# Shifting the lower weight parts of an MLP's first product by 224 bytes in SBUF

## The chip, the cores and the metric

The kernel runs on one core of one Trainium2 chip. The metric is device time in microseconds (us), from the start to the end of one execution. Before the change three runs gave a median of 1940.86 us (1940.85 to 1940.98).

## The reference

The program is a trunk of two layers on 256 tokens with 2048 features, in float32. Layer 0 mixes tokens with a convolution module, layer 1 with multi-head latent attention. Each mixer is followed by an MLP with squared ReLU; every sub-layer has an RMS norm ahead of it and a residual add behind it, and one last RMS norm ends the program.

```python
for layer in range(DEPTH):                       # DEPTH = 2
    h = rms_norm(x, norm_mixer_g[layer])
    x = x + (conv_module if layer % 2 == 0 else mla)(h, ...)
    h = rms_norm(x, norm_mlp_g[layer])
    x = x + jnp.square(jax.nn.relu(h @ w1)) @ w2  # w1: 2048 x 8192, w2: 8192 x 2048
return rms_norm(x, final_norm_g)
```

The change is about `h @ w1`, the up product of the MLP, which both layers compute.

## The kernel before

**Products in parts.** A float32 product is made from one-pass matmuls in the type float32r. Each operand is split into a higher part (the value rounded by a copy to float32r, on ScalarE) and a lower part (the value minus the higher part, on VectorE or GpSimd). Three products are added: higher by higher, lower by higher, higher by lower. The tiles of the weights' parts are called `hi` and `lo`; there are six buffers of each (`WB`), in one pool, 4096 bytes per partition each. A matmul has a stationary operand, which a weight load (LDWEIGHTS, PEld in the profile) brings into the array ahead of it, and a moving operand that streams through. The profile names them in the order moving, stationary: `acc<-xt,lo` streams tokens past lower weight parts.

**The up product** (lines 487 to 520) runs on weights that arrive in units of 128 columns and all 2048 rows, 8192 bytes per partition. A unit is cut into two chunks of eight blocks of 128 x 128. For each block the weights are stationary and the tokens move: one matmul with `hi` on 512 columns (line 510: the tokens' higher and lower parts stand side by side in the tiles `xt`), and one with `lo` on the 256 columns of the tokens' higher parts (line 508). The first chunk of a unit runs its eight `hi`, then its eight `lo`; the second chunk its eight `lo`, then its eight `hi`. So sixteen `lo` matmuls follow each other, then eight `hi`, then the next work. Each layer has 64 such units; a layer's count of matmuls on line 508 is 1024, on line 510 also 1024.

**The down product** has the activations stationary and the weight parts `hi` and `lo` moving, 512 columns at a time (`mm3`, lines 195 to 197). `stream` (from line 423) runs over the chunks of both products in an order written out beforehand. For each chunk it first prepares parts up to six chunks ahead (`prep`, which calls `split_into`, lines 420 and 421), then issues the matmuls. When a raw unit has been read by its last split, the next load starts. TensorE, ScalarE and VectorE work in the order of this code.

**The other places.** The convolution's first product (lines 850 to 852) has `hi` and `lo` stationary and 256 token columns moving. The down projection of attention streams 288 columns of `hi` and `lo` at a time past the tokens. `turn` (line 288) loads small vectors (norm gains, biases) by transposing staged rows and copying the result out of PSUM into `vecs` and `vecs2`. `rsqrt`, `finish` and others take small tiles from the pool `small`, which has two buffers of each unless told otherwise.

**Where the tiles lie.** Several narrow tiles named `pad_...` serve only to place what follows them. In the built program the tiles that matmuls in float32r read (`hi`, `lo`, `xt`, the activations' `sh` and `sl`, the parts in attention) all begin at 64 modulo 256 bytes in their partition, and so does each block of 128 x 128 in them, since a block is 512 bytes. Only the second half of the 288 moving columns in attention's down projection begins at 192.

Of the kernel before, what the change touches and what calls it, by code (L numbers as in the profile page):

```python
# [10 lines left out]
F32 = mybir.dt.float32  # L11
F32R = mybir.dt.float32r
# [6 lines left out]
P = 128  # L19
D = 2048  # L20
KC = D // P
T = 2
S = T * P
FF = 4 * D
NB = 512
NNB = D // NB
# [6 lines left out]
QR = 512  # L33
# [1 line left out]
CHUNK = 64  # L35
PARTS = 4
PAD_CONST = 24
PAD_SMALL = 32
PAD_RIGHT = 40
PAD_SH = 16  # L40
PAD_STATS = 48
PAD_O = 64
WB = 6
# [39 lines left out]
def trunk_kernel(  # L83
# [29 lines left out]
    const = ctx.enter_context(tc.tile_pool(name="const", bufs=1))  # L113
    main = ctx.enter_context(tc.tile_pool(name="main", bufs=1))
    wpool = ctx.enter_context(tc.tile_pool(name="wpool", bufs=2))
    small = ctx.enter_context(tc.tile_pool(name="small", bufs=2))
    psum, psum_cx = {}, [ExitStack()]

    def repool(name, **banks):
# [19 lines left out]
    def nm(s):  # L139
        uid[0] += 1  # L140
        return f"{s}_{uid[0]}"
# [70 lines left out]
    def rsqrt(ms, n, eps, name):  # L212

        v = small.tile([P, n], F32, tag=f"v{name}", name=nm("v"))
        y = small.tile([P, n], F32, tag=f"y{name}", name=nm("y"))
        t = small.tile([P, n], F32, tag=f"t{name}", name=nm("t"))
        nc.vector.tensor_scalar(v, ms, scalar1=eps, scalar2=None, op0=ALU.add)
        nc.scalar.activation(t, v, AF.Sqrt)
        nc.vector.reciprocal(y, t)
        nc.vector.scalar_tensor_tensor(out=t, in0=y, scalar=-0.5, in1=y, op0=ALU.mult, op1=ALU.mult)  # L220
        nc.vector.tensor_tensor(t, t, v, op=ALU.mult)
        nc.vector.scalar_tensor_tensor(out=y, in0=t, scalar=1.5, in1=y, op0=ALU.add, op1=ALU.mult)
        return y
# [61 lines left out]
            at += r  # L285
        return stage

    def turn(dst, stage):
        n = dst.shape[-1]
        pt = tr_tile()  # L290
        nc.tensor.transpose(pt[:, :n], stage[:n, :], ident[:n, :n])
        nc.vector.tensor_copy(dst, pt[:, :n])

    n_vecs, n_vecs2 = (sum(r for _, r in v) for v in (vec_rows, vec_rows2))
    vecs = const.tile([P, n_vecs], F32, name="vecs")
    vecs2 = const.tile([P, n_vecs2], F32, name="vecs2")
    g_mix = [vecs[:, 0:KC], vecs[:, KC : 2 * KC]]
    g_mlp = [vecs[:, 2 * KC : 3 * KC], vecs[:, 3 * KC : 4 * KC]]
    b_pw1 = vecs[:, 4 * KC : 6 * KC]
    b_dw = vecs[:, 6 * KC : 7 * KC]  # L300


    xt_cx, xt = [ExitStack()], []
# [24 lines left out]
    def residual_stage(last, gain, r_scale=None):  # L328


        ssq = small.tile([P, T, NNB], F32, tag="ssq", name=nm("ssq")) if last else None

        def add(n, ps, t):
            sl = slice(n * NB, (n + 1) * NB)
            if r_scale is None:
                nc.vector.tensor_tensor(xs[:, t, sl], ps[t], xs[:, t, sl], op=ALU.add)
            else:
                nc.vector.scalar_tensor_tensor(
                    out=xs[:, t, sl], in0=ps[t], scalar=r_scale[:, t : t + 1], in1=xs[:, t, sl],
                    op0=ALU.mult, op1=ALU.add,  # L340
                )

        def prepare(n, only=None):
            sl = slice(n * NB, (n + 1) * NB)
            if last:
                if gain is not None:
                    for j in range(2):
                        to_T(xs, 4 * n + 2 * j, xh, xl, gain)
                for t in range(T) if only is None else [only]:
                    nc.scalar.activation(spare[-1](), xs[:, t, sl], AF.Square, accum_out=ssq[:, t, n : n + 1])  # L350

        return ssq, add, prepare
# [60 lines left out]
        def __init__(self, prep, run, after=(), now=None, ahead=None):  # L413
            self.prep, self.run, self.after, self.now, self.ahead = prep, run, after, now, ahead

    def hi_lo(n):
        return [wpool.tile([P, n, NB], F32R, tag=c, name=nm(c), bufs=WB) for c in ("hi", "lo")]

    def split_into(parts, src):
        nc.scalar.activation(parts[0], src, AF.Copy)  # L420
# [53 lines left out]
    def mlp(layer, ssq, next_gain, finish=None, before=None, last_w1=None):  # L474

        w1, w2 = mlp_w1[layer], mlp_w2[layer]
        r2 = small.tile([P, T], F32, tag="r2", name=nm("r2"))
        made_stage, pre, first_tiles, blocked, n_s, sums_left = [], [], {}, {}, [0], []

        def u_tile():  # L480
# [5 lines left out]
        def up_units(hs, q, p, extra):  # L486

            sevens = SEVENS[layer][q]
            held = {}
            large = p in sevens or (q == PARTS - 1 and p in LATE_G[layer])  # L490

            def up_unit(b):
                ps = []

                def chunk(h):
                    def prep(raw, parts):
                        parts[h] = [a.rearrange("p a (j n) -> p (a j) n", n=P) for a in hi_lo(2)]
                        split_into(parts[h], raw[:, 8 * h : 8 * h + 8, :])

                    def run(parts):  # L500
                        if not ps:
                            ps.append(acc_tile())
                        wh, wl = parts.pop(h)
                        for low in (h, 1 - h):
                            for j in range(8):
                                k = 8 * h + j
                                if low:
                                    nc.tensor.matmul(ps[0][:, :S], wl[:, j, :], xh(k), start=False, stop=False)  # L508
                                else:
                                    nc.tensor.matmul(ps[0], wh[:, j, :], xhl(k), start=k == 0, stop=k == KC - 1)  # L510

                    def out():
                        if b == 0:
                            held["u"] = u_tile()
                        nc.scalar.activation(held["u"][:, b, :], ps[0], AF.Copy)  # L515

                    if h == 0:
                        return Chunk(prep, run)
                    return Chunk(prep, run, [add, lambda: None, square, forms, part] + extra if b == 1 else [], now=out)

                unit = Unit(rows(w1, 0, KC, ((q * NPAIR + p) * 2 + b) * P, P), KC, [chunk(h) for h in range(2)])
                unit.last_read = 1
                return unit

            def add():
                v = held["u"][:, :, :S]
                nc.vector.tensor_tensor(v, v, held["u"][:, :, S:], op=ALU.add)

            def square():
                n_s[0] += large  # L530
                v = held["u"][:, :, :S]
                nc.scalar.activation(v, v, AF.Relu)
                if p in sevens:
                    held["f"] = f = f_tile()
                    nc.scalar.activation(f[:, 0:4, :].rearrange("p (b t) n -> p b (t n)", b=2), v, AF.Square)
                    held["src"], shape, tag, n = f[:, 1:8, :], [P, 7, P], "s", N_S
                else:
                    nc.scalar.activation(v, v, AF.Square)
                    held["src"], shape = v, [P, 2, S]
                    tag, n = ("s", N_S) if large else ("g", N_G)  # L540
                held["hl"] = [mp.tile(shape, F32R, tag=tag + c, name=nm(tag + c), bufs=n) for c in "hl"]

            def forms():
                if p in sevens:
                    f = held["f"]
                    nc.vector.tensor_tensor(
                        f[:, 4:6, :], f[:, 0:1, :].broadcast_to([P, 2, P]), f[:, 1:3, :], op=ALU.subtract
                    )
                    nc.vector.tensor_tensor(f[:, 6, :], f[:, 1, :], f[:, 5, :], op=ALU.subtract)
                    nc.vector.tensor_tensor(f[:, 7, :], f[:, 3, :], f[:, 6, :], op=ALU.subtract)  # L550

            def part():
                hs[p] = held["hl"]
                split_into(hs[p], held["src"])

            if large:
                blocked[square] = lambda: n_s[0] < N_S and not (p in sevens and sums_left)
            return [up_unit(b) for b in range(2)]
# [235 lines left out]
    with ExitStack() as cx:  # L794
# [2 lines left out]
        squares_to = cv.tile([P, NB], F32, name="squares_to")  # L797
        spare.append(lambda: squares_to)

        ln_g = vecs2[:, 0:KC]  # L800
        ln_b = vecs2[:, KC : 2 * KC]
        g_q = vecs2[:, 2 * KC : 2 * KC + QR // P]
        g_kv = vecs2[:, 2 * KC + QR // P :]
        NW = W * KC // 4
        w_dw = cv.tile([P, W * KC], F32, name="w_dw")
        vecs_rows = stage_rows(cv, vec_rows, nc.scalar)
# [1 line left out]
        b2 = cv.tile([P, D], F32, name="b2")  # L808

        cn = cv.tile([P, T, D], F32, tag="tok", name="cn")  # L810
        cv.tile([P, PAD_SH], F32, name="pad_sh")
        sh = cv.tile([P, KC, S], F32R, name="sh")
        sl_ = cv.tile([P, KC, S], F32R, name="sl_")
        cv.tile([P, PAD_STATS], F32, name="pad_stats")
# [202 lines left out]
        with tc.manual_schedule():  # L1017
# [8 lines left out]
                nc.scalar.activation(xn[:, 1, hs], xs[:, 1, hs], AF.Square, accum_out=xsq[:, h : h + 1])  # L1026
            for n in range(NNB):
                nc.vector.bn_stats(xst[:, n, :], xs[:, 0, n * NB : (n + 1) * NB])
            turn(vecs, vecs_rows)
            keep_warm(xs[:, 1, D - P :], N_WARM)  # L1030
            nc.vector.bn_aggr(xmv, xst.rearrange("p a b -> p (a b)"))
            nc.vector.tensor_tensor(ms0[:, 0:1], xmv[:, 0:1], xmv[:, 0:1], op=ALU.mult)
# [31 lines left out]
            turn0(3)  # L1064
            conv_mm(0, 4)
            conv_load(4)
            turn(vecs2, vecs2_rows)
            conv_mm(0, 8)
            pt = tr_tile()
            for i in range(4):  # L1070
# [672 lines left out]
    def before(ssq):  # L1743

        for t in range(T):
            m = small.tile([P, 1], F32, tag="msp", name=nm("msp"))
            nc.vector.tensor_reduce(m, ssq[:, t, : NNB // 2], axis=AX.X, op=ALU.add)
            nc.vector.tensor_scalar(m, m, scalar1=1.0 / D, scalar2=EPS, op0=ALU.mult, op1=ALU.add)
            part.append(m)
# [30 lines left out]
```

## Time and profile before

| | |
|---|---|
| median of three runs | 1940.86 us (1940.85 to 1940.98) |
| profiled execution | 1940.68 us, span 1938.9 us |
| granted TensorE clock, mean | 0.998 |
| matmuls, weight loads | 10778 each |
| line 510, `hi`, 512 columns | 2048 |
| line 508, `lo`, 256 columns | 2048 |

The profiled execution's own time is 0.18 us under the median; 1.8 us of it lie outside the span, which goes from the first to the last instruction. A matmul's duration in the profile is modelled and overlaps that of the next, so the cost of one in a row of matmuls is the distance from its start to the next start, called its pitch here. The shapes in a row are partitions x elements, "idle" is the time that the engine stood still just ahead of the group.

### The profile page before, as it was taken

What the parts mean: (1) busy time and instruction counts of PE and PEld (TensorE: products, weight loads), DVE (VectorE), ACT (ScalarE), POOL (GpSimd) and SP (SyncE); (2) the same over time, 40 slices, a digit from 0 to 9 for tenths busy, and PEclk for the clock granted to TensorE, in tenths of its full rate; (3) what the DMA queues carried; (4) which work ended last, traced back from release to release, by engine and by line L of the source; (5) the groups of instructions that cost most, each with busy time, mean ns of one, the idle gap of its engine ahead of it and who ended that gap; (6) DMA issues with size and microseconds to landing.
All of it is one profiled execution on the core that took longest, in us unless ns stands there. A gap on an engine that the chain in (4) does not pass through costs nothing.

```text
span 1938.9 us, 28476 instructions
## 1 busy us (share of the span) xinstructions
PE 1915.4 (99%) x10778; PEld 1682.5 (87%) x10778; DVE 1651.8 (85%) x2372; ACT 1204.8 (62%) x1709; POOL 223.7 (12%) x183
## 2 busy tenths in 40 slices
PE   7999999999999999999999999999999999999998
PEld 7999888888888888888899998888888888888886
DVE  5999875789999999999976666557999999999887
ACT  5556654766666666666566665556766666666654
POOL 5999400000000000000001410000000000000000
PEclk9999999999999999999999999999999999999999
DMA  8666456857666667666646445765667666766663
GB/s 236 184 175 177 146 184 169 222 171 210 198 204 204 203 198 212 200 198 212 199 143 182 121 152 174 200 186 171 201 191 210 210 196 195 214 200 195 211 223 109
DMA packets 407113, 367.62 MB, mean 190 GB/s; under 512 B 15416, under 2 KB 351936, under 8 KB 406720
## 3 DMA queue, kind: packets, MB, share of 16 engines
q1 hardware_dynamic: 405952, 363.63, 62.8%
q10 hardware_dynamic: 1024, 2.17, 0.3%
q8 instruction: 84, 1.38, 0.3%
q14 instruction: 53, 0.43, 0.1%
HBM read 363.68 MB, written 2.10 MB: 189 GB/s over the span
## 4 chain that ended last, share of the span: by engine, by line
PE 98%; DVE 1%; DMA 1%; ACT 0%; issue 0%; DVEq 0%; ACTq 0%
PE acc L510 24%; PE acc L196 15%; PE acc L195 15%; PE acc L197 15%; PE acc L508 13%; PE acc L851 3%; PE acc L850 3%; PE acc L852 3%; PE acc L251 1%; PE sum L900 1%; PE acc L1435 0%; PE acc L1437 0%; PE acc L1436 0%; PE acc L1412 0%; PE acc L1414 0%; PE acc L1413 0%
## 5 line engine op out<-in xcount | busy, mean ns | idle before, releaser
L421 DVE TENSOR_TENSOR lo<-raw,hi 128x1024 fp32r<-128x1024 f32 (+1 forms) x512 | 571.1, 1122 | 90.1 <-ACT hi L420 81.7
L420 ACT ACTIVATE hi<-raw 128x1024 fp32r<-128x1024 f32 (+1 forms) x512 | 479.7, 970 | 66.9 <-PE acc L196 66.6
L510 PE MATMUL acc<-xt,hi 128*128 128x512 f32 x2048 | 503.2, 391 | 0.0
L510 PEld LDWEIGHTS acc<-xt,hi 128*128 128x128 f32 x2048 | 376.1, 188 | 72.5
L195 PE MATMUL acc<-hi,sh 128*128 128x512 f32 x930 | 362.7, 390 | 0.0
L197 PE MATMUL acc<-lo,sh 128*128 128x512 f32 x930 | 362.0, 389 | 0.0
L196 PE MATMUL acc<-hi,sl 128*128 128x512 f32 x802 | 312.0, 389 | 0.0
L508 PEld LDWEIGHTS acc<-xt,lo 128*128 128x128 f32 x2048 | 262.6, 191 | 10.0
L508 PE MATMUL acc<-xt,lo 128*128 128x256 f32 x2048 | 265.7, 283 | 0.0
L169 ACT ACTIVATE hi<-raw 128x1024 fp32r<-128x1024 f32 (+2 forms) x184 | 179.8, 1005 | 46.8 <-PE acc L196 43.0
L197 PEld LDWEIGHTS acc<-lo,sh 128*128 128x128 f32 x930 | 174.6, 188 | 36.2
L195 PEld LDWEIGHTS acc<-hi,sh 128*128 128x128 f32 x930 | 174.6, 188 | 36.0
L170 DVE TENSOR_TENSOR lo<-raw,hi 128x1024 fp32r<-128x1024 f32 (+2 forms) x118 | 132.8, 1146 | 68.5 <-ACT hi L169 62.8
L420 ACT ACTIVATE hi<-V 128x1024 fp32r<-128x1024 f32 x94 | 99.5, 1059 | 129.6 <-DVE V L716 114.8
L196 PEld LDWEIGHTS acc<-hi,sl 128*128 128x128 f32 x802 | 150.5, 188 | 31.2
L952 DVE SCALAR_TENSOR_TENSOR sum<-ub,w_dw,sum 128x256 f32<-128x256 f32 x400 | 163.3, 482 | 8.7 <-ACT sum L908 7.1
L170 POOL TENSOR_TENSOR lo<-raw,hi 128x1024 fp32r<-128x1024 f32 x66 | 157.7, 2409 | 24.4 <-ACT hi L169 24.4
L420 ACT ACTIVATE hi<-T 128x1024 fp32r<-128x1024 f32 x94 | 99.2, 1056 | 89.6 <-DVE T L704 77.2
L515 ACT ACTIVATE U<-acc 128x512 f32<-128x512 f32 x128 | 76.0, 593 | 117.6 <-PE acc L510 117.0
L850 PE MATMUL acc<-xt,hi 128*128 128x256 f32 x512 | 146.3, 286 | 0.0
L851 PE MATMUL acc<-xt,hi 128*128 128x256 f32 x512 | 145.0, 283 | 0.3 <-DVE xt L208 0.3
L852 PE MATMUL acc<-xt,lo 128*128 128x256 f32 x512 | 144.9, 283 | 0.0
(269 smaller groups left out, 2805.5 us busy)
## 6 DMA issues: line engine op xcount, KB each, us to landing
raw<-in_mlp_w SPq DMA_DIRECT2D x256, 1024.0 KB, 6.1
raw<-in_conv_w_pw SPq DMA_DIRECT2D x64, 512.0 KB, 5.5
raw<-in_conv_w_pw SPq DMA_DIRECT2D x16, 1024.0 KB, 5.1
raw<-in_mla_w_o SPq DMA_DIRECT2D x16, 1024.0 KB, 5.3
raw<-in_mla_w_kv_up SPq DMA_DIRECT2D x8, 1024.0 KB, 5.4
raw<-in_mla_w_in SPq DMA_DIRECT2D x8, 576.0 KB, 3.8
raw<-in_mla_w_in SPq DMA_DIRECT2D x4, 1024.0 KB, 7.1
raw<-in_mla_w_q_up SPq DMA_DIRECT2D x16, 256.0 KB, 5.1
```

What stands on the lines that cost most here:

```text
L169: nc.scalar.activation(hi, raw[:, js, :], AF.Copy)
L170: eng.tensor_tensor(lo, raw[:, js, :], hi.bitcast(F32), op=ALU.subtract)
L195: nc.tensor.matmul(ps, sh, mh, start=start, stop=False)
L196: nc.tensor.matmul(ps, sl, mh, start=False, stop=False)
L197: nc.tensor.matmul(ps, sh, ml, start=False, stop=stop)
L420: nc.scalar.activation(parts[0], src, AF.Copy)
L421: nc.vector.tensor_tensor(parts[1], src, parts[0].bitcast(F32), op=ALU.subtract)
L508: nc.tensor.matmul(ps[0][:, :S], wl[:, j, :], xh(k), start=False, stop=False)
L510: nc.tensor.matmul(ps[0], wh[:, j, :], xhl(k), start=k == 0, stop=k == KC - 1)
L850: nc.tensor.matmul(o, wh[:, bs], xh(k), start=k == 0, stop=False)
L851: nc.tensor.matmul(o, wh[:, bs], xl(k), start=False, stop=False)
L852: nc.tensor.matmul(o, wl[:, bs], xh(k), start=False, stop=k == KC - 1)
```

## The change

The `lo` buffers become 256 bytes longer (`LO_GAP` is 64 floats). `hi_lo` takes an offset at which the lower part begins in its buffer. For the up product it is 56 floats, 224 bytes; for the down product 0. The convolution's and attention's own splits (`split_half`) still take `lo` tiles of the plain length. Space for the longer buffers is found elsewhere: most small tiles have one buffer instead of two, and the vectors that only the convolution reads (two biases, the layer norm's gain and bias) move from `vecs` and `vecs2` into the convolution's own pool, as `vecs_cv` and `vecs2_cv`. `turn` now copies one transposed block into two tiles. The pads are adjusted.

```diff
-PAD_SMALL = 32
+PAD_VECS = 16
+PAD_SMALL = 8
 PAD_RIGHT = 40
-PAD_SH = 16
+LO_GAP = 64
...
-    small = ctx.enter_context(tc.tile_pool(name="small", bufs=2))
+    small = ctx.enter_context(tc.tile_pool(name="small", bufs=1))
...
-    def turn(dst, stage):
-        n = dst.shape[-1]
+    def turn(dsts, stage):
+        n = sum(dst.shape[-1] for dst in dsts)
         pt = tr_tile()
         nc.tensor.transpose(pt[:, :n], stage[:n, :], ident[:n, :n])
-        nc.vector.tensor_copy(dst, pt[:, :n])
+        at = 0
+        for dst in dsts:
+            nc.vector.tensor_copy(dst, pt[:, at : at + dst.shape[-1]])
+            at += dst.shape[-1]
...
-    def hi_lo(n):
-        return [wpool.tile([P, n, NB], F32R, tag=c, name=nm(c), bufs=WB) for c in ("hi", "lo")]
+    def hi_lo(n, at=0):
+        hi = wpool.tile([P, n, NB], F32R, tag="hi", name=nm("hi"), bufs=WB)
+        lo = wpool.tile([P, n * NB + LO_GAP], F32R, tag="lo", name=nm("lo"), bufs=WB)
+        return [hi, lo[:, at : at + n * NB].rearrange("p (a b) -> p a b", b=NB)]
...
-                        parts[h] = [a.rearrange("p a (j n) -> p (a j) n", n=P) for a in hi_lo(2)]
+                        parts[h] = [a.rearrange("p a (j n) -> p (a j) n", n=P) for a in hi_lo(2, LO_GAP - 8)]
...
-            turn(vecs, vecs_rows)
+            turn((vecs, vecs_cv), vecs_rows)
...
-            turn(vecs2, vecs2_rows)
+            turn((vecs2_cv, vecs2), vecs2_rows)
```

In the built program the buffers of `hi` and `lo`, `xt` and the activations' parts still begin at 64 modulo 256. The up product's lower parts begin 224 bytes later, at 32 modulo 256: 32 bytes below the phase of the tokens that stream past them. Outside the float32r matmuls some tiles change their place modulo 256: the convolution's `xn` and `cn` go from 0 to 64, its taps `w_dw` from 64 to 128.

The order of instructions on TensorE, ScalarE, GpSimd and the DMA queue is the same as before. On VectorE the start of the program reads, before (`tr` is the PSUM tile of the transpose, `xst`, `xmv`, `ms` and `v` the statistics of the first norm):

```order
L1028 BN_STATS xst<-xs 128x6 x4
L292 COPY vecs<-tr_160 128x112
L1031 BN_AGGR xmv<-xst 128x2
L1032 TENSOR_TENSOR ms_153<-xmv 128x1
L1033 TENSOR_TENSOR ms_153<-ms_153,xmv 128x1
```

and after:

```order
L1036 BN_STATS xst<-xs 128x6 x4
L295 COPY vecs<-tr_162 128x64
L295 COPY vecs_cv<-tr_162 128x48
L1039 BN_AGGR xmv<-xst 128x2
L1040 TENSOR_TENSOR ms_155<-xmv 128x1
L1041 TENSOR_TENSOR ms_155<-ms_155,xmv 128x1
```

One copy of 112 columns has become two, of 64 and 48; the statistics stand behind both. The same happens later to the copy of 40 columns, which becomes 32 and 8.

More of the change, by code (lines that the diff above doesn't have):

```diff
@@ L214, in rsqrt @@
         v = small.tile([P, n], F32, tag=f"v{name}", name=nm("v"))
-        y = small.tile([P, n], F32, tag=f"y{name}", name=nm("y"))
+        y = small.tile([P, n], F32, tag=f"y{name}", name=nm("y"), bufs=2)
         t = small.tile([P, n], F32, tag=f"t{name}", name=nm("t"))
@@ L286, in stage_rows @@
         return stage
-    def turn(dst, stage):
-        n = dst.shape[-1]
+    def turn(dsts, stage):
+        n = sum(dst.shape[-1] for dst in dsts)
         pt = tr_tile()
         nc.tensor.transpose(pt[:, :n], stage[:n, :], ident[:n, :n])
-        nc.vector.tensor_copy(dst, pt[:, :n])
+        at = 0
+        for dst in dsts:
+            nc.vector.tensor_copy(dst, pt[:, at : at + dst.shape[-1]])
+            at += dst.shape[-1]
     n_vecs, n_vecs2 = (sum(r for _, r in v) for v in (vec_rows, vec_rows2))
-    vecs = const.tile([P, n_vecs], F32, name="vecs")
-    vecs2 = const.tile([P, n_vecs2], F32, name="vecs2")
+    vecs = const.tile([P, 4 * KC], F32, name="vecs")
+    vecs2 = const.tile([P, n_vecs2 - 2 * KC], F32, name="vecs2")
+    const.tile([P, PAD_VECS], F32, name="pad_vecs")
     g_mix = [vecs[:, 0:KC], vecs[:, KC : 2 * KC]]
     g_mlp = [vecs[:, 2 * KC : 3 * KC], vecs[:, 3 * KC : 4 * KC]]
-    b_pw1 = vecs[:, 4 * KC : 6 * KC]
-    b_dw = vecs[:, 6 * KC : 7 * KC]
     xt_cx, xt = [ExitStack()], []
@@ L328, in residual_stage @@
     def residual_stage(last, gain, r_scale=None):
-        ssq = small.tile([P, T, NNB], F32, tag="ssq", name=nm("ssq")) if last else None
+        ssq = small.tile([P, T, NNB], F32, tag="ssq", name=nm("ssq"), bufs=2) if last else None
         def add(n, ps, t):
@@ L476, in mlp @@
         w1, w2 = mlp_w1[layer], mlp_w2[layer]
-        r2 = small.tile([P, T], F32, tag="r2", name=nm("r2"))
+        r2 = small.tile([P, T], F32, tag="r2", name=nm("r2"), bufs=2)
         made_stage, pre, first_tiles, blocked, n_s, sums_left = [], [], {}, {}, [0], []
@@ L798, in trunk_kernel @@
         spare.append(lambda: squares_to)
[L800 to L803, printed above, removed]
+        vecs_cv = cv.tile([P, n_vecs - 4 * KC], F32, name="vecs_cv")
+        vecs2_cv = cv.tile([P, 2 * KC], F32, name="vecs2_cv")
+        b_pw1 = vecs_cv[:, 0 : 2 * KC]
+        b_dw = vecs_cv[:, 2 * KC : 3 * KC]
+        ln_g = vecs2_cv[:, 0:KC]
+        ln_b = vecs2_cv[:, KC : 2 * KC]
+        g_q = vecs2[:, 0 : QR // P]
+        g_kv = vecs2[:, QR // P :]
         NW = W * KC // 4
@@ L810, in trunk_kernel @@
         cn = cv.tile([P, T, D], F32, tag="tok", name="cn")
-        cv.tile([P, PAD_SH], F32, name="pad_sh")
         sh = cv.tile([P, KC, S], F32R, name="sh")
@@ L1745, in before @@
         for t in range(T):
-            m = small.tile([P, 1], F32, tag="msp", name=nm("msp"))
+            m = small.tile([P, 1], F32, tag="msp", name=nm("msp"), bufs=2)
             nc.vector.tensor_reduce(m, ssq[:, t, : NNB // 2], axis=AX.X, op=ALU.add)
```

## The prediction

> **What bounds the kernel now.** I read the page first: the busy shares, the granted clock and the chain that ended last.
>
> ```profile
> span 1938.9 us, 28476 instructions
> ...
> PE 1915.4 (99%) x10778; PEld 1682.5 (87%) x10778; DVE 1651.8 (85%) x2372; ACT 1204.8 (62%) x1709; POOL 223.7 (12%) x183
> ...
> PEclk9999999999999999999999999999999999999999
> ...
> PE 98%; DVE 1%; DMA 1%; ACT 0%; issue 0%; DVEq 0%; ACTq 0%
> PE acc L510 24%; PE acc L196 15%; PE acc L195 15%; PE acc L197 15%; PE acc L508 13%; PE acc L851 3%; PE acc L850 3%; PE acc L852 3%; PE acc L251 1%; PE sum L900 1%; PE acc L1435 0%; PE acc L1437 0%; PE acc L1436 0%; PE acc L1412 0%; PE acc L1414 0%; PE acc L1413 0%
> ```
>
> The chain is 98% TensorE at full clock, so the time is the number of matmuls times their pitch, from start to start. Then the groups of the lines that the change touches: the up product's matmuls on the higher (L510) and lower (L508) weight parts, and the split that writes the lower parts (L421).
>
> ```profile
> L421 DVE TENSOR_TENSOR lo<-raw,hi 128x1024 fp32r<-128x1024 f32 (+1 forms) x512 | 571.1, 1122 | 90.1 <-ACT hi L420 81.7
> ...
> L510 PE MATMUL acc<-xt,hi 128*128 128x512 f32 x2048 | 503.2, 391 | 0.0
> ...
> L508 PEld LDWEIGHTS acc<-xt,lo 128*128 128x128 f32 x2048 | 262.6, 191 | 10.0
> L508 PE MATMUL acc<-xt,lo 128*128 128x256 f32 x2048 | 265.7, 283 | 0.0
> ```
>
> Neither group of matmuls waits (0.0 us idle). "Mean ns" of a matmul is modelled and overlaps the next one, so the pitch is taken from start times. The timeline of TensorE in the first MLP, where up units follow each other, gives it:
>
> ```profile
> 322.60 2.08 PE L508 MATMUL acc<-xt,lo 128*128 128x256 f32 x16
> 324.51 3.82 PE L510 MATMUL acc<-xt,hi 128*128 128x512 f32 x16
> 328.17 2.08 PE L508 MATMUL acc<-xt,lo 128*128 128x256 f32 x16
> 330.08 3.82 PE L510 MATMUL acc<-xt,hi 128*128 128x512 f32 x16
> 333.73 2.08 PE L508 MATMUL acc<-xt,lo 128*128 128x256 f32 x16
> ```
>
> Sixteen L508 take 324.51 - 322.60 = 1.91 us, 119.4 ns each; sixteen L510 take 3.66 us, 228.8 ns each. 128 such runs of sixteen (two layers, 64 column blocks) make the 2048. The run isn't even. The same group view in five short windows (first L508 of a run; its later ones; the first two L510 behind it; the first eight; the next nine) shows it in the modelled duration, which moves with the pitch:
>
> ```profile
> L508 PE MATMUL acc<-xt,lo 128*128 128x256 f32 x1 | 0.3, 278 | 0.0
> ...
> L508 PE MATMUL acc<-xt,lo 128*128 128x256 f32 x14 | 1.8, 283 | 0.0
> ...
> L510 PE MATMUL acc<-xt,hi 128*128 128x512 f32 x2 | 0.6, 397 | 0.0
> ...
> L510 PE MATMUL acc<-xt,hi 128*128 128x512 f32 x8 | 2.0, 392 | 0.0
> ...
> L510 PE MATMUL acc<-xt,hi 128*128 128x512 f32 x9 | 2.2, 389 | 0.0
> ```
>
> The first L508 is 5 ns shorter than those that follow it, and the first two L510 behind a run are 8 ns longer than settled ones, with the same operands, no wait and an even clock. What differs is only how the weight load and the token stream stand against each other in time. That is the thing that a shifted address can move. More on it, again from start times: two stretches of 512-column matmuls (settled; then from the second matmul behind an interruption by transposes), first and last row of each.
>
> ```profile
> 234.67 0.39 PE L195 MATMUL acc<-hi,sh 128*128 128x512 f32 x1
> ...
> 238.08 0.39 PE L195 MATMUL acc<-hi,sh 128*128 128x512 f32 x1
> ...
> 239.44 0.40 PE L196 MATMUL acc<-hi,sl__120 128*128 128x512 f32 x1
> ...
> 241.29 0.39 PE L195 MATMUL acc<-hi,sh 128*128 128x512 f32 x1
> ```
>
> Settled, 15 pitches take 3.41 us (227 ns); behind the interruption 8 take 1.85 us (231 ns). With 256 columns (settled in the convolution; behind an interruption in attention), and with 288 columns (the third pair, the down projection of attention):
>
> ```profile
> 20.26 0.28 PE L850 MATMUL acc<-xt,hi 128*128 128x256 f32 x1
> ...
> 22.30 0.28 PE L852 MATMUL acc<-xt,lo 128*128 128x256 f32 x1
> ...
> 1074.70 0.28 PE L196 MATMUL acc<-kTh,qTl 128*128 128x256 f32 x1
> ...
> 1075.53 0.28 PE L195 MATMUL acc<-hi,qh 128*128 128x256 f32 x1
> ...
> 994.36 0.29 PE L195 MATMUL acc<-hi,xt 128*128 128x288 f32 x1
> ...
> 997.15 0.29 PE L195 MATMUL acc<-hi,xt 128*128 128x288 f32 x1
> ```
>
> Settled, 17 pitches take 2.04 us (120.0 ns); behind the interruption 7 take 0.83 us (118.6 ns). So with 512 columns the settled state is the cheap one (227 against 231), with 256 the dear one (120.0 against 118.6). Between 256 and 512 columns the settled pitch grows by 107 ns, 0.418 ns a column; what does not scale with the columns is 120 - 107 = 13 ns. This 13 ns is what a better or worse address could change.
>
> **The change, part by part.** (1) The 256 lower parts of the up product start at 32 modulo 256 instead of 64, while tokens (xt) and higher parts stay at 64. TensorE's order and the number of instructions stay. It touches 2048 weight loads, each beside the matmul ahead of it. No row shows a one-pass matmul (fp32r) with operands 32 bytes apart, so I bound the price per L508. Gain: the first L508's 278 against 283 ns is the nearest row below, 5 ns x 2048 = 10.2 us; if moreover the eight L510 behind each run lose their 392 - 389 = 3 ns, 128 x 8 x 3 = 3.1 us more, 13.3 us together. Loss: 8 ns, as the first L510 pay (397 against 389), x 2048 = 16.4 us. The attention stretch off its settled state, 118.6 against 119.4 here, gives only 0.8 x 2048 = 1.6 us. I take half of the first gain, 2.5 ns x 2048 = 5.1 us, because the stretches of 256 columns that are off their settled state read lower and not higher, and half of the 3.1 us behind the runs, 1.5 us. Together -6.6 us.
>
> (2) The vector of gains is copied out of PSUM in two pieces at the start, and again later in two pieces.
>
> ```profile
> 12.26 3.19 PE L234 MATMUL acc<-ident,xs 128*128 128x128 f32 x14
> ...
> 12.50 0.27 DVE L292 COPY vecs<-tr 128x112 f32<-128x112 f32 x1 [2.06 <-PE tr L291]
> 12.70 0.25 DVE L1031 BATCH_NORM_AGGREGATE xmv<-xst 128x2 f32<-128x24 f32 x1
> ...
> 14.72 3.26 DVE L1041 TENSOR_SCALAR xn<-xs,y 128x512 f32<-128x512 f32 x8
> ...
> 15.26 0.18 PEld L251 LDWEIGHTS tr<-ident,xn 128*128 128x128 f32 x1 [0.21 <-DVE xn L1041]
> ```
>
> The copy takes a slot of 0.20 us on VectorE (12.50 to 12.70), and the first transposes wait for that engine (0.21 us). A second copy delays all behind it by up to 0.20 us, and I add 0.2 in full. The later pair stands in the convolution, where TensorE works from its backlog; if that cover were gone it would cost the same 0.2.
>
> (3) Small tiles become single. Each is rewritten by an engine that stands in order behind its earlier use (statistics of two norms, the final norm's pair of token halves): 0; were one to wait, it would be for one such small instruction, 0.25 us at most by the row of 12.70. Gains and biases at other places: the same instructions read them, 0.
>
> (4) VectorE writes the shifted parts. Its slack in the MLP is read from the busy time by window:
>
> ```profile
> 322.60:1000.00 677.40, 677.40 (x3492) 581.92 (x3491) 618.28 (x750) 436.72 (x549) 0.15 (x1) 1.00 0.65 194
> ```
>
> VectorE is busy 618.28 of 677.40 us: 59 us free, 460 ns for each of the layer's 128 shifted splits of 1122 ns. Anything under that stays hidden, as six buffers stand between split and matmul: 0.
>
> Sum: -6.6 + 0.2 = -6.4 us on the profiled execution's 1940.68 us, 1934.3. Its span is 1938.9 with 1.8 us around it, and it stands 0.2 us under the runs' median, 1940.86; so 1934.5 us for the median.
>
> **The rivals.** *Nothing changes (1941.1 us).* The 13 ns might belong to every one-pass matmul, whatever the addresses. For it: the 288-column row. There the tokens are weights and the moving columns alternate, three matmuls each, between the same phase and 128 bytes beyond it; 21 pitches take 2.79 us, 132.9 ns, and 120.0 + 32 x 0.418 = 133.4 would be expected with no effect at all. Also these transposes:
>
> ```profile
> L251 PE MATMUL acc<-ident,xs 128*128 128x128 f32 x96 | 12.5, 273 | 0.2
> ...
> L990 PE MATMUL tr<-ident,ca 128*128 128x128 f32 x28 | 5.3, 272 | 0.0
> ```
>
> In L990 the weights (ca, at 192) stand 32 bytes below the moving tile (ident, at 224), just as in the change; in L251 (xs, at 64) 160 below: 272 and 273 ns. Against it: transposes run at the slower pace of full fp32, and the 5 to 8 ns above do move with the phase in time. The time would be 1940.86 + 0.2. The Trainium skill speaks for this rival: "SBUF — State Buffer", section "Who interferes with whom", gives TensorE two read ports, one for the moving operand and one for weight loads, independent of each other, and says that it waits for nobody. By that rule no address relation can matter, and the sum would be the +0.2 us alone. The trace agrees in the two rows just shown and not in the pitches that vary with no wait.
>
> *The new phase is a worse one (1947 us, up to 1957).* If 32 bytes put the loads of lower parts where the first L510 behind a run stand now, each L508 becomes longer: by the mean excess of the eight L510, 3 ns x 2048 = 6.1 us, 1947.2 with the 0.2; by 8 ns, 1957.5. It decides once an L508 run takes more than 1.91 us, and slower by 0.2% (3.9 us, which I take as what a measurement of this kernel tells from no change) from 1.8 ns per L508. For it: 512-column stretches off their settled state are dearer. Against it: with 256 columns they are cheaper.
>
> *VectorE becomes the bound.* Writing at 32 would have to cost over 460 ns per split before TensorE waits all through; nothing shows such a write.
>
> In a sentence apart: the Trainium skill, "TensorE: Matmul & The Clock Gate", section "Back-to-back issue gap", gives N / 2.4 + 2.5 ns for an isolated pitch, 109 ns at 256 columns; an estimate from that page alone would put the most that L508 can gain at about 10 ns x 2048 = 21 us, which no run here shows.
>
> **How the numbers follow.** Faster through a cheaper phase 0.45, nothing changes 0.25, worse phase 0.29, VectorE 0.01. The first case's own range is 1927.5 (-13.3) to 1939.5 (-1.6 + 0.2); nearly all of it lies beyond 0.2%, and the part within is offset by the part of the second that a small gain would push beyond. So faster 0.45, same 0.25, slower 0.30. The range reaches from 1927, the bound of the gain, to 1950, which takes in the milder worse phase and leaves out the 8 ns end: about 0.05 below and 0.13 above. The likeliest case gives 1934.5.
>
> **What would show it.** Right: an L508 run from its first start to the next L510 under 1.91 us (1.87 by my sum), L510 behind it nearer to 389 than 392 ns, everything else of equal pitch. Wrong: runs of 1.91 us with equal L510 (nothing changes), or L508 above 283 ns and runs above 1.91 us (worse phase). Idle time ahead of L508, released by VectorE's lo, would point to the write. The first transpose should start 0.2 us later.

## The result, and the profile after

The changed kernel takes 1935.89 us, the median of 9 runs (1935.74 to 1936.0); the kernel before, on the same chip, takes 1940.92 us (1940.75 to 1940.98). That is 5.0 us less, a ratio of 0.9974 with a 95% interval of 0.9966 to 0.9983. The profiled execution is one of 1935.74 us.

In the changed kernel the up product's matmuls stand on line 513 (`lo`, line 508 before) and line 515 (`hi`, 510 before), the split on 425 and 426, the copies of `turn` on 295, the convolution's first product on 858 to 860. The page of the profile of the changed kernel: span, busy times, granted clock, the chain that ended last, then the groups of the split, of `hi` and of `lo` (busy us, mean ns of one, idle us ahead of them).

```profile
span 1933.9 us, 28479 instructions
...
PE 1910.2 (99%) x10778; PEld 1676.2 (87%) x10778; DVE 1651.6 (85%) x2374; ACT 1204.9 (62%) x1709; POOL 224.0 (12%) x183
...
PEclk9999999999999999999999999999999999999999
...
PE 98%; DVE 1%; DMA 1%; ACT 0%; issue 0%; DVEq 0%; ACTq 0%
...
L426 DVE TENSOR_TENSOR lo<-raw,hi 128x1024 fp32r<-128x1024 f32 (+1 forms) x512 | 571.8, 1124 | 88.0 <-ACT hi L425 87.7
...
L515 PE MATMUL acc<-xt,hi 128*128 128x512 f32 x2048 | 504.0, 391 | 0.0
...
L513 PE MATMUL acc<-xt,lo 128*128 128x256 f32 x2048 | 259.8, 279 | 0.0
```

The chain is TensorE as before, at full clock. The busy time of `lo` falls from 265.7 to 259.8 us (5.9 less), that of `hi` rises from 503.2 to 504.0 (0.8 more). Together 5.1 us, the whole difference. The split costs 2 ns more (1122 before), and the idle time ahead of it is still released by ScalarE.

TensorE's timeline in the first MLP of the changed kernel (start, duration):

```profile
322.72 2.03 PE L513 MATMUL acc<-xt,lo 128*128 128x256 f32 x16
324.58 3.82 PE L515 MATMUL acc<-xt,hi 128*128 128x512 f32 x16
328.24 2.03 PE L513 MATMUL acc<-xt,lo 128*128 128x256 f32 x16
330.11 3.82 PE L515 MATMUL acc<-xt,hi 128*128 128x512 f32 x16
```

Sixteen `lo` take 1.86 to 1.87 us instead of 1.91. To see what happens at both ends of a run, I take the same group view in three short windows: the last `hi` ahead of a run, the four that are in flight from the first one behind it, and the settled ones. Before:

```profile
L510 PE MATMUL acc<-xt,hi 128*128 128x512 f32 x1 | 0.4, 389 | 0.0
...
L510 PE MATMUL acc<-xt,hi 128*128 128x512 f32 x4 | 1.1, 394 | 0.0
...
L510 PE MATMUL acc<-xt,hi 128*128 128x512 f32 x9 | 2.2, 389 | 0.0
```

After:

```profile
L515 PE MATMUL acc<-xt,hi 128*128 128x512 f32 x1 | 0.4, 396 | 0.0
...
L515 PE MATMUL acc<-xt,hi 128*128 128x512 f32 x4 | 1.1, 394 | 0.0
...
L515 PE MATMUL acc<-xt,hi 128*128 128x512 f32 x9 | 2.2, 390 | 0.0
```

The last `hi` ahead of a run has become 7 ns longer (389 to 396); the ones behind it are as long as they were (394). The nine of the third window take in the last one ahead of the next run, which makes their mean 390 instead of 389. The start times of the trace give this exactly. Averaged over the 126 runs that have eight `hi` on either side:

| pitch, ns | before | after |
|---|---|---|
| last `hi` ahead of the run | 226.7 | 235.0 |
| the run of sixteen `lo` | 1912.5 (119.5 each) | 1865.0 (116.6 each) |
| first five `hi` behind it | 233.3 235.8 228.3 232.5 230.8 | 232.5 235.8 228.3 232.5 230.8 |
| eight `hi`, sixteen `lo`, eight `hi` | 5566.7 | 5526.7 |

The run gains 47.5 ns, its entry loses 8.3, its exit gains 0.8. That is 40 ns for each of 128 runs, 5.1 us.

### The profile page after: what moved, and what is told of

It reads as the page before. It is cut to its first block, busy times and chain, and to the rows that moved or that the text cites. A ratio compares the mean times of both kernels' runs of the same rounds, so it can differ in the third digit from the quotient of the medians.

```text
span 1933.9 us, 28479 instructions
## 1 busy us (share of the span) xinstructions
PE 1910.2 (99%) x10778; PEld 1676.2 (87%) x10778; DVE 1651.6 (85%) x2374; ACT 1204.9 (62%) x1709; POOL 224.0 (12%) x183
## 4 chain that ended last, share of the span: by engine, by line
PE 98%; DVE 1%; DMA 1%; ACT 0%; issue 0%; DVEq 0%; ACTq 0%
PE acc L515 24%; PE acc L196 15%; PE acc L197 15%; PE acc L198 15%; PE acc L513 12%; PE acc L859 3%; PE acc L858 3%; PE acc L860 3%; PE acc L252 1%; PE sum L908 1%; PE acc L1443 0%; PE acc L1445 0%; PE acc L1444 0%; PE acc L1420 0%; PE acc L1421 0%; PE acc L1422 0%
## 5 line engine op out<-in xcount | busy, mean ns | idle before, releaser
L426 DVE TENSOR_TENSOR lo<-raw,hi 128x1024 fp32r<-128x1024 f32 (+1 forms) x512 | 571.8, 1124 | 88.0 <-ACT hi L425 87.7
L515 PE MATMUL acc<-xt,hi 128*128 128x512 f32 x2048 | 504.0, 391 | 0.0
L513 PEld LDWEIGHTS acc<-xt,lo 128*128 128x128 f32 x2048 | 257.7, 188 | 10.9
L513 PE MATMUL acc<-xt,lo 128*128 128x256 f32 x2048 | 259.8, 279 | 0.0
L860 PE MATMUL acc<-xt,lo 128*128 128x256 f32 x512 | 144.9, 283 | 0.0
```

The lines of the kernel that those rows point to most:

```text
L426: nc.vector.tensor_tensor(parts[1], src, parts[0].bitcast(F32), op=ALU.subtract)
L860: nc.tensor.matmul(o, wl[:, bs], xh(k), start=False, stop=k == KC - 1)
```

## The experiments

Each is the changed kernel with the edit shown. The one number that most of them vary is how far the up product's lower parts (the weights) begin from the tokens, modulo 256 bytes: 0 before, -32 in the change. The texts on record name the theories that they compare: that the relation of the two addresses sets the pitch, that the lower parts' own place does, or that something else in the change does.

### The shift taken back, everything else kept

```diff
-... hi_lo(2, LO_GAP - 8)]
+... hi_lo(2, 0)]
```

> The changed kernel with the lower parts of the up product back at 64 modulo 256; the longer buffers, the single small tiles and the split copies stay. Theory A (the relation between the addresses of weights and tokens sets the pitch): runs of sixteen lower matmuls back at 1.91 us, 1941.1 us in all, which is the kernel before plus 0.2 us for the split copy at the start. Theory C (another part of the change gave the gain): runs of 1.87 us or a gain elsewhere, about 1936 us.

Measured: 1940.83 us (11 runs, 1940.66 to 1941.04) against 1940.78 for the kernel before, ratio 1.0 (0.9991 to 1.0009). Its groups of `hi` and `lo` on the page:

```profile
L515 PE MATMUL acc<-xt,hi 128*128 128x512 f32 x2048 | 503.2, 391 | 0.0
...
L513 PE MATMUL acc<-xt,lo 128*128 128x256 f32 x2048 | 265.7, 283 | 0.0
```

Both are those of before to the digit. The shift alone makes the gain; longer buffers, single small tiles, the split copy and the moved vectors cost or bring nothing that these runs can tell.

### Other distances: +32, +128, -64, +96, -96, -16

Only the offset differs: 8, 32, `LO_GAP - 16`, 24, 40 and `LO_GAP - 4` floats.

```diff
-... hi_lo(2, LO_GAP - 8)]
+... hi_lo(2, 8)]               # +32
+... hi_lo(2, 32)]              # +128
+... hi_lo(2, LO_GAP - 16)]     # -64
+... hi_lo(2, 24)]              # +96
+... hi_lo(2, 40)]              # -96
+... hi_lo(2, LO_GAP - 4)]      # -16
```

> Lower parts 32 bytes above the tokens' phase instead of 32 below (offset 32 bytes instead of 224). Theory A with any difference that is no multiple of 128 being as good: 116.6 ns per lower matmul, 1935.9 us. Theory A with a sign: 120 ns or more, 1941 us or more, since the load then runs into the token stream from the other side. Theory B (what counts is that the lower parts lie at 32 modulo 64, whatever the tokens do): 116.6 ns, 1935.9 us, as 96 is 32 modulo 64 too.

> Lower parts 128 bytes above the tokens' phase. Theory A, going by the 288-column matmuls of attention's down projection, half of which stand 128 apart and cost as much as the others: 119.4 to 120 ns per lower matmul, 1941 us. If the period is 256 bytes and only the relation 0 is dear: 116 to 117 ns, 1936 us. Theory B: 120 ns (192 is 0 modulo 64), 1941 us.

> Lower parts 64 bytes below the tokens' phase (offset 192 bytes). Theory A1 (a weight load that stands further below the tokens stays clear of them for longer, so that below is better than above): 116 ns or less per lower matmul, 1935 us or less. Theory A2 (32 bytes matters because it is half of 64, and multiples of 64 are alike): 119.5 to 120.3 ns, as with 0 and +128, 1941 us.

> Lower parts 96 bytes above the tokens' phase, which is 32 below modulo 128. If the pattern repeats every 128 bytes (0 and +128 took the same time): 116.6 ns per lower matmul, 1935.9 us. If it repeats only every 256 bytes: some other value, by the others 117 to 120 ns, 1937 to 1942 us.

> Lower parts 96 bytes below the tokens' phase (offset 160 bytes), which is 32 above modulo 128. If the pattern repeats every 128 bytes: as with +32, 118.2 ns per lower matmul, 512-column matmuls behind the run disturbed for eight and more, about 1941.7 us. If below is what matters: near 117 ns and 1936 to 1937 us.

> Lower parts 16 bytes below the tokens' phase (offset 240 bytes). Theory A1: between 0 and -32, about 118 ns per lower matmul and 1938 to 1939 us. Theory A2: unlike 0 as 16 is no multiple of 64: 116 to 118 ns, 1936 to 1939 us; 119.5 ns and 1941 us would say that 16 bytes are too small a step to matter.

> The kernel with the lower parts 16 below once more, since its one execution ran at a clock of 0.655 from start to end. If that clock was an event of that moment: full clock, 116 to 119 ns per lower matmul, 1936 to 1941 us. If the 16 bytes bring it about: 0.655 and about 2730 us again.

The first execution at -16 took 2731.54 us. The page of that execution shows why it tells nothing of the edit:

```profile
span 2729.8 us, 28479 instructions
...
PEclk7666666666666666666666666666666666666666
```

The granted clock was about two thirds of full speed throughout; the same kernel later ran seven times at full clock, 1935.79 us (1935.76 to 1935.96), ratio 0.9974 (0.9963 to 0.9985). What lowered the clock in that one execution stays open.

The groups of `hi` and `lo` on the pages of the other distances, first +32:

```profile
L515 PE MATMUL acc<-xt,hi 128*128 128x512 f32 x2048 | 506.5, 393 | 0.0
...
L513 PE MATMUL acc<-xt,lo 128*128 128x256 f32 x2048 | 262.9, 281 | 0.0
```

+128:

```profile
L515 PE MATMUL acc<-xt,hi 128*128 128x512 f32 x2048 | 502.0, 391 | 0.0
...
L513 PE MATMUL acc<-xt,lo 128*128 128x256 f32 x2048 | 266.9, 284 | 0.0
```

-64:

```profile
L515 PE MATMUL acc<-xt,hi 128*128 128x512 f32 x2048 | 506.9, 392 | 0.0
...
L513 PE MATMUL acc<-xt,lo 128*128 128x256 f32 x2048 | 262.1, 279 | 0.0
```

+96:

```profile
L515 PE MATMUL acc<-xt,hi 128*128 128x512 f32 x2048 | 503.5, 391 | 0.0
...
L513 PE MATMUL acc<-xt,lo 128*128 128x256 f32 x2048 | 261.2, 280 | 0.0
```

-96:

```profile
L515 PE MATMUL acc<-xt,hi 128*128 128x512 f32 x2048 | 503.6, 391 | 0.0
...
L513 PE MATMUL acc<-xt,lo 128*128 128x256 f32 x2048 | 266.5, 282 | 0.0
```

-16, the later runs:

```profile
L515 PE MATMUL acc<-xt,hi 128*128 128x512 f32 x2048 | 503.1, 391 | 0.0
...
L513 PE MATMUL acc<-xt,lo 128*128 128x256 f32 x2048 | 260.8, 279 | 0.0
```

Together, with the pitches from the start times (ns; the whole is the time of eight `hi`, sixteen `lo`, eight `hi`; the times at -64, -96, +128, +96 and +32 are of one execution each):

| distance | one `lo`, mean | last `hi` ahead | whole | time, us |
|---|---|---|---|---|
| 0 (before; shift taken back) | 119.5 | 226.7 | 5566.7 | 1940.9 |
| -16 | 117.1 | 226.7 | 5526.8 | 1935.8 |
| -32 (the change) | 116.6 | 235.0 | 5526.7 | 1935.9 |
| -64 | 117.8 | 225.9 | 5568.6 | 1941.9 |
| -96 | 120.1 | 236.6 | 5580.0 | 1942.6 |
| +128 | 120.3 | 232.5 | 5566.9 | 1941.0 |
| +96 | 117.3 | 228.3 | 5533.4 | 1936.8 |
| +32 | 118.2 | 235.0 | 5570.8 | 1941.7 |

Two things follow. First, the run itself is cheaper at five of the seven distances other than 0: dear among those tried are 0, +128 and -96. A rule that sorts the distances doesn't show; the effect doesn't repeat every 128 bytes (+32 gives 118.2, -96 gives 120.1). Second, the run isn't all. At +32 and -64 it gains 21 and 28 ns, and the `hi` around it lose that again: their group grows by 3.3 and 3.7 us. At -64 the `hi` behind the run take between 224 and 241 ns, and where sixteen follow each other they settle at 226.7 only from the eleventh on; in the kernel before it was the sixth. A distance is worth something only if the 512-column matmuls keep their cheap state, as they do at -16, -32 and +96.

### The tokens moved in place of the weights

```diff
-PAD_RIGHT = 40
+PAD_RIGHT = 32
...
-... hi_lo(2, LO_GAP - 8)]
+... hi_lo(2, 0)]
```

`xt` now begins at 96, all weight parts at 64: the distance is -32 for `lo`, for `hi` and for the convolution's weights.

> The tokens move instead of the weights: the tiles xt begin at 96 modulo 256, all weight parts at 64. The weights stand 32 below the tokens for the lower and the higher parts of the up product and for the convolution's first product. Theory A: runs of lower matmuls near 1.87 us, convolution matmuls (1536, 256 columns) from 120 to about 117 ns, that is 5 us in the MLP and up to 5 us in the convolution; the higher parts with 512 columns, whose settled state looked like the cheap one, may lose up to 4 ns x 2048 = 8 us. Theory B: lower parts at 120 ns, nothing gained, 1941 us.

Measured: 1945.41 us, one execution. The page of this kernel:

```profile
L515 PE MATMUL acc<-xt,hi 128*128 128x512 f32 x2048 | 512.8, 395 | 0.0
...
L513 PE MATMUL acc<-xt,lo 128*128 128x256 f32 x2048 | 261.4, 280 | 0.0
...
L858 PE MATMUL acc<-xt,hi 128*128 128x256 f32 x512 | 144.6, 282 | 0.0
```

`lo` lies where it lay before and gains 4.3 us (265.7 to 261.4), so its own place isn't the cause; the distance to the tokens is. The convolution's matmuls gain too: their pitches, without the waits among and behind them, sum to 181.6 instead of the 186.2 us of the kernel with the shift taken back. But `hi`, at -32 as well, loses 9.6 us (503.2 to 512.8): with 512 columns this distance costs 233.3 ns each on average, instead of 226.7 settled. That fits the price at the entry of a run in the change (235.0): there a `hi` streams while the first `lo` is loaded. So -32 is good beside 256 columns and bad beside 512.

### The distance for `lo` and for the convolution, with `hi` at 0

The higher parts get the longer buffers and begin at 96, as the tokens do; `lo` and the convolution's weights stay at 64.

```diff
-PAD_RIGHT = 40
-LO_GAP = 64
+PAD_RIGHT = 32
+HI_GAP = 64
...
-        hi = wpool.tile([P, n, NB], F32R, tag="hi", name=nm("hi"), bufs=WB)
-        lo = wpool.tile([P, n * NB + LO_GAP], F32R, tag="lo", name=nm("lo"), bufs=WB)
-        return [hi, lo[:, at : at + n * NB].rearrange("p (a b) -> p a b", b=NB)]
+        hi = wpool.tile([P, n * NB + HI_GAP], F32R, tag="hi", name=nm("hi"), bufs=WB)
+        lo = wpool.tile([P, n, NB], F32R, tag="lo", name=nm("lo"), bufs=WB)
+        return [hi[:, at : at + n * NB].rearrange("p (a b) -> p a b", b=NB), lo]
...
-... hi_lo(2, LO_GAP - 8)]
+... hi_lo(2, 8)]
```

> The tokens at 96 modulo 256, lower parts at 64, the up product's higher parts moved along to 96 (the 256 spare bytes go to their buffers instead). So every matmul of 256 token columns in the up product and in the convolution has its weights 32 below the tokens, and every one of 512 stays at relation 0. Theory A: the up product as in the changed kernel, the convolution's 1536 matmuls at 117 to 118 ns as with the tokens moved alone, 3.8 us less; the attention projections that now hold tokens as weights lose up to 1.5 us: 1932.5 to 1934 us. If the gain of the lower parts needs the higher parts at 64, 1937 us or more.

Measured: 1938.72 us (11 runs, 1938.29 to 1940.42) against 1940.85, ratio 0.9991 (0.9982 to 1.0). The convolution settles at 117 ns and `lo` is as in the change, but `hi` grows:

```profile
L515 PE MATMUL acc<-xt,hi 128*128 128x512 f32 x2048 | 507.1, 392 | 0.0
...
L513 PE MATMUL acc<-xt,lo 128*128 128x256 f32 x2048 | 259.8, 279 | 0.0
```

The sixteen `lo` of a run have the pitches of the change, one by one to 0.1 ns (118.3, 117.5, 115.8 and so on), though tokens and weights lie 32 bytes further up here (96 and 64) than there (64 and 32). This shows more plainly than the page that the distance counts and not the places.

What grows isn't the settled `hi`. Where sixteen `hi` stand between two runs, 39 of the 42 such stretches settle at 226.7 ns as in the change, with weights and tokens both at 96. The loss stands where the up product (`hi` and tokens at 96) and the down product (operands at 64) meet. Mean pitches at these seams, from start times; in the change all of them are 226.7:

| seam | last matmul ahead of it | the next ones, in order |
|---|---|---|
| up to down product (74) | 235.0 | 230.0 235.8 228.3 232.5 230.8 226.6 |
| down to up product (84) | 235.0 | 230.0 224.2 230.8 235.8 228.3 232.5 230.8 |

The last matmul ahead of a seam has its own weights at distance 0 and still takes 235.0; only what comes next lies elsewhere. It is the 235.0 of the last `hi` ahead of a run in the change, where of the next matmul the weights alone have moved. Their load begins 3 ns behind the start of that last `hi` (328.012 and 328.009 us in the change's trace). So the distance that counts for a matmul is most likely the one between the tile that it streams and the weights that are loaded meanwhile, those of the next matmul. Five or more matmuls with 512 columns follow before the pitch is settled again.

Against the change the seams cost `hi` 3.2 us and the down product 2.5 us. The convolution's matmuls gain 4.7 us. New waits among and behind them took 1.7 us of that in the profiled execution. Behind the last of these waits the clock was lowered, which cost another 1.7 us (the next kernel shows the same).

### The change, with the convolution's tokens moved alone

The convolution has tokens of its own, so they can be moved without the MLP's.

```diff
-    def open_xt(name):
+    def open_xt(name, pad=0):
...
+        if pad:
+            pool.tile([P, pad], F32, name=nm("pad_xt"))
...
-    open_xt("xt0")
+    open_xt("xt0", 56)
...
+        open_xt("xtm")
```

The convolution's `xt` begin at 96, the MLP's at 64 again. Lines from here on are two further down: the convolution's matmuls 860 to 862, its last channel's taps 910 instead of 908.

> The changed kernel, and besides the convolution's own token tiles at 96 modulo 256, while its weight parts stay at 64 (32 below). For the MLP the tiles are opened anew at 64, so that nothing else moves. Theory A (256-column matmuls off the relation 0 are cheaper, and no 512-column matmul is disturbed): convolution matmuls at 117 ns instead of 120 as with the tokens moved everywhere, 1536 x 2.5 to 3 ns, 1931.5 to 1932.5 us. Rival: opening the tiles anew adds a wait at the end of the convolution, 1936 us or more.

Measured: 1934.02 us (5 runs, 1932.6 to 1934.17) against 1940.91, ratio 0.9963 (0.9949 to 0.9977); the profiled execution is one of 1933.99. It is the best version so far, 1.9 us under the change, but the expectation asked for 3.4 at least. Of the rival, a wait at the tiles opened anew, the list of TensorE's waits has nothing. The view of one line, the 44 matmuls of the last channel's taps, shows where the rest went. In the change (min/median/max ns, first and last start):

```profile
L908 PE MATMUL sum<-ub,dg x44: 377/378/484, 209.8 to 219.4; 128*128 128x256 f32 x44
```

Here, followed by the busy times of two short windows (length, busy us of PE, PEld, DVE, ACT, POOL with their counts, then the granted clock, the DMA share and GB/s):

```profile
L910 PE MATMUL sum<-ub,dg x44: 377/379/792, 206.4 to 217.7; 128*128 128x256 f32 x44
```

```profile
206.40:208.00 1.60, 1.60 (x4) 1.32 (x5) 1.60 (x5) 1.60 (x5) 1.60 (x1) 0.50 0.04 10
208.00:210.00 2.00, 2.00 (x7) 1.59 (x6) 2.00 (x6) 1.98 (x3) 1.92 (x4) 0.56 0.00 0
```

The taps begin 3.4 us earlier, as they should (209.8 to 206.4), but end only 1.7 us earlier: the clock was 0.50 and 0.56 for the first 3.6 us. They wait for VectorE's `ub`, and that wait is longer now that TensorE arrives sooner, 2.06 us against 1.15.

### That gap filled

Fourteen transposes of the identity stand in the gap (1.69 us), in the tile that the taps write after them.

```diff
                 last_sum.append(o)
+                for i in range(14):
+                    nc.tensor.transpose(o[:, i % 2 * P : (i % 2 + 1) * P], ident, ident)
                 last_products(0, LAST_PE // 2)
```

> The kernel with the convolution's tokens moved (e9, 1934.02 us) lost time at its last channel: TensorE stood still for 2.06 us before the taps (L910, 206.4 us), the granted clock of the windows 206.4 to 208 and 208 to 210 was 0.50 and 0.56, and the 44 taps took 11.3 us instead of 9.6. Here 14 transposes of the identity into the taps' own PSUM tile stand in that gap (8 of them take 0.87 us in the rows of that trace, so some 1.5 us), and nothing else changes. Theory A (the idle time lowers the clock, and the lower clock is what the taps cost): clock 1.00 in both windows, taps 9.6 us, the program 1.5 to 1.7 us shorter, 1932.4 us. Theory B (the taps are slow by something else, such as the places of ub and dg, or the sums on VectorE set the end of this stage anyway): taps 11.3 us or the same end of the stage, 1934.0 us. If the transposes end after the last channel's input is there, they cost up to their 1.5 us.

Measured: 1932.41 us (5 runs, 1932.29 to 1932.86) against 1940.8, ratio 0.9958 (0.9944 to 0.9971). The taps and the two windows of this kernel:

```profile
L910 PE MATMUL sum<-ub,dg x44: 377/378/483, 206.3 to 215.9; 128*128 128x256 f32 x44
```

```profile
206.40:208.00 1.60, 1.60 (x8) 1.41 (x9) 1.60 (x5) 1.60 (x5) 1.60 (x1) 1.00 0.00 0
208.00:210.00 2.00, 2.00 (x11) 1.76 (x10) 2.00 (x6) 1.89 (x2) 1.92 (x4) 1.00 0.00 0
```

Work that computes nothing made the program 1.6 us shorter, by keeping the clock up. With it the program is shorter than the change by the 3.5 us by which the taps begin earlier. This version, 8.4 us under the kernel before, is the fastest of all that were run.

## Why the prediction was right

1934.5 us was forecast and 1935.89 measured, inside the range and on the side of the likeliest case.

**Part (1), the gain of the run.** 2.5 ns for each `lo` was taken, half of the bound of 5 ns, 5.1 us. Measured are 3.0 ns (1912.5 to 1865.0 over sixteen), 6.1 us. The run took 1.87 us, the number that the prediction named as the sign. The choice rested on 256-column stretches being cheaper off their settled state; five of the seven distances agree with it, -96 and +128 don't. That reason says nothing of the distance and would have forecast the same gain at all seven. At four of them (+32, +128, -64, -96) eight `hi`, sixteen `lo`, eight `hi` take as long as before or longer. That -32 is among the good ones was luck. That the address alone can make the run cheaper was right; that it does so by the phase of load and stream in time, as the prediction has it, is not shown.

**Part (1), the 1.5 us behind the runs.** This term failed. The eight `hi` behind a run kept their dear start, 27 ns altogether, and did not come nearer to 389. It isn't lifted by leaving 0: at -32 and -16 it is there to within 0.8 ns a run, at +96 in full; only at +128 is it down to some 10 ns (`hi` 502.0 us on its page). In its place stands a cost that the prediction didn't have, 8.3 ns at the last `hi` ahead of each run, 128 x 8.3 = 1.1 us. The prediction said that the load stands beside the matmul ahead of it, and had the row that 512 columns react the other way; it did not put the two together for the one `hi` that streams beside a load of `lo`. The seams between the up and the down product show the same 235.0 ns. The two halves of part (1) together: 6.1 - 1.1 + 0.1 = 5.1 us, where 6.6 was forecast. The total came so near because the run gave 1.0 us more than was taken for it.

**Part (2), the split copy.** The start on VectorE after the change reads:

```profile
12.56 0.22 DVE L295 COPY vecs<-tr 128x64 f32<-128x64 f32 x1 [2.10 <-PE tr L292]
12.70 0.20 DVE L295 COPY vecs_cv<-tr 128x48 f32<-128x48 f32 x1
12.81 0.25 DVE L1039 BATCH_NORM_AGGREGATE xmv<-xst 128x2 f32<-128x24 f32 x1
```

The statistics start 0.25 us behind the first copy instead of 0.20, since the two shorter copies take slots of 0.14 and 0.11. So 0.05 us there where 0.2 was allowed. The sign that was named, a first transpose 0.2 us later, nearly came: it starts 2.92 us behind the first copy instead of 2.76, 0.16 later. Where the other 0.11 us come from stays open, and nothing of it is left at the end. The sum of the program with this copy and no shift differs from before by 0.05 us, less than its scatter.

**Parts (3) and (4)** were put at nothing, and the kernel with everything but the shift, and the 1124 ns split with no wait of TensorE for `lo`, bear that out.

**The rivals.** "Nothing changes" fell: the transposes spoke for it, and they run at another pace. The 288-column row couldn't have told, since it compared 0 with 128 bytes, and these two are alike at 256 columns as well (119.5 and 120.3 ns). The Trainium skill, "SBUF — State Buffer", section "Who interferes with whom", would have it so too, with two independent read ports; the runs contradict the conclusion drawn from it, since the distance of two addresses moves the pitch by up to 3.7 ns in 120 with no wait (116.6 at -32, 120.3 at +128). Whether the ports or something behind them is the cause, no run here shows. "A worse phase" didn't come about at -32 for `lo`, but it exists: -96 is slower than before by 1.7 us, and the whole set of tokens at 96 by 4.6. VectorE was never the bound.

## What to carry to other kernels

Where a chain is all TensorE with no waits, the place of weights and moving tiles modulo 256 bytes can still be worth something (2.4% of one line's pitch here). Look at each moving tile together with the weights that are loaded while it streams, those of the next matmul, also where one product hands over to another; try some distances for each count of columns apart, and judge by the pitch from start to start of the matmuls around the moved ones too, as the neighbours can lose what the moved ones gain. Make one execution with only the shift taken back, so that the rest of such a change is priced. When a stage gets faster, look at the gap that it now opens ahead of the next one, and at the granted clock behind that gap.

## What the runs showed that I had not expected

- The effect has the opposite sign for 256 and 512 columns at one distance: -32 brings 256 columns from 119.5 to 116.6 ns and 512 columns from 226.7 to 233.3 (all tokens moved).
- At -32 a run never becomes even: from its third matmul on the pitch goes 115.8, 117.5, 120.0, 113.3 and round again. At 0 it is 120.0 throughout once settled.
- A gap of about 2 us on TensorE can be enough to lower the clock. Behind gaps of 2.06 and 2.04 us it was 0.50 for 3.41 us in the profiled executions of two kernels (the convolution's tokens moved alone; the distance for `lo` and for the convolution). In the kernel with the tokens moved in place of the weights the same line waited 2.05 us, and its 44 taps took 9.7 us from the first start to the last, against 9.6 in the change. The times of the first two kernels fall into two groups 1.4 to 1.6 us apart (1932.6 and 1934.0 to 1934.2; 1938.3 to 1938.7 and 1940.0 to 1940.4), which fits a gap that sometimes lowers the clock and sometimes not; with the gap filled to 0.54 us all five runs lay in the lower group. What decides is perhaps where the gap falls: in both traces the low clock began 191.15 us after the clock's record first shows full speed, 56 times 3.41 us. Counted in such steps, 2.02 and 2.04 us of the two gaps lie within one step. In the third kernel a step begins inside the gap (204.73, gap from 204.50 to 206.55) and 1.82 us lie in one. No run tests this. The Trainium skill, "TensorE: Matmul & The Clock Gate", section "HAM oscillation — how this bites in real kernels", asks for no gap over about 3.4 us; here 2.06 us was enough in one execution.
